# Scan tables of the next layer made by another engine, small vector instructions merged, and norm factors spread by transposes in a two-layer hybrid decoder kernel

## The chip, the cores and the metric

The kernel runs on one core of one Trainium2 chip. The metric is the device time of one execution in microseconds (us); less is better. TensorE (PE) multiplies matrices, VectorE (DVE), ScalarE (ACT) and GpSimd (POOL) work on tiles of up to 128 partitions, SyncE (SP) issues most transfers. Durations of single instructions are in nanoseconds (ns) where marked.

## The reference

The program is the trunk of a decoder with two layers, for one sequence of 512 tokens and a model width of 1024. Each layer adds to x a mixer and a feed-forward.

- The mixer projects RMSNorm(x) once, and slices of this projection feed three groups: six NSA heads (compressed, selected and windowed attention), six MLA heads, and a state-space scan (S5) with 16 groups of 16 channels and 64 complex states each. The groups are normed, concatenated and projected back.
- The feed-forward multiplies by an up matrix (1024 x 5632), convolves the gate half over three tokens, and multiplies by a down matrix (2816 x 1024).

What the change touches, cut down:

```python
def rms_norm(x, g):
    y = x * lax.rsqrt(jnp.mean(x * x, axis=-1, keepdims=True) + EPS)
    return y * g

def compress_blocks(blocks, pe, w1, b1, w2, b2):       # k and v of NSA, 31 blocks of 32 tokens
    h = gelu(einsum('bnlkd,ldf->bnkf', blocks + pe[:, None, :], w1) + b1)
    return einsum('bnkf,fd->bnkd', h, w2) + b2

def s5_ssm(u, log_dt, a_re, a_im, b_re, b_im, c_re, c_im, d, w_glu, b_glu):
    a_bar = exp(a * dt)                                # the scan tables hold powers of a_bar
    b_bar = ((a_bar - 1.0) / a)[..., None] * (b_re + 1j * b_im)
    h = scan(a_bar, einsum('bsgc,gpc->bsgp', u, b_bar))
    y = einsum('bsgp,gcp->bsgc', h, c).real + d * u
    z = gelu(y)
    return z * sigmoid(z @ w_glu + b_glu)

def conv_ffn(h, w_up, conv_w, conv_b, w_down):
    gate, val = split(h @ w_up, 2)
    gate = sum(pad(gate)[:, k:k + S] * conv_w[k] for k in range(3)) + conv_b
    return (silu(gate) * val) @ w_down
```

## The kernel before

Features lie on partitions and the 512 tokens on the free axis, so a projection tile is 128 features by 512 tokens in one PSUM bank. Each fp32 product is made of three passes (`mm3`, lines 240 to 242): a weight is split into a high part (a cast on ScalarE, line 226) and a low part (a subtraction on POOL or VectorE, line 227), and so is the activation. `wload` (line 234) loads a weight tile on SP's queue, with three raw buffers and four split ones.

In a layer the mixer's tasks (projections, the tables, the compression, the heads, the scan) are issued by a table (PLAN0 for layer 0, PLAN1 for layer 1), and the framework's scheduler makes each engine's final order from it, by its own estimate of times. An engine runs its instructions in that order. Tiles of 128x512 in SBUF come from an arena with three areas (main, side, aux) in which a name's number is a slot.

Names and lines that matter here:

- `rstd_` (to line 271) computes one norm factor for each token, as a column of 128 tokens for each of four blocks. It spreads each column over 128 partitions by a matmul of the column, broadcast, with the identity. `rstd_` is called 16 times, 14 times with four blocks and twice with two.
- `ssm_params` (lines 396 ff.) makes the scan's tables for a quarter of the scan's groups. Its complex product `cm` takes three lines: L425 (product with the real part), L426 (product with the imaginary part) and L427 (their sum), each 128x512. The tables of layer 0 are made inside its mixer; those of layer 1 in layer 0's feed-forward, two quarters in its first group (about 404 to 444 us) and two in its second (about 571 to 592 us).
- `ssm_spill` (lines 430 ff.) makes the convolution kernel of a quarter: transposes (L440), products (L447), a copy from PSUM by ScalarE (L451), and L453, which adds d on the diagonal of four 16x16 blocks.
- `compress` (for v) forms the gelu of the hidden layer six times over (L841, 128x31 each), multiplies by w2, adds a bias (L846) and multiplies by head masks (L850, 128x64 each).
- L519 are the score matmuls of a head, in four blocks of rows, L520 VectorE's instruction that takes a block out of its bank, adds the mask and finds the extremum of each row (with a short read of the accumulator behind it); the softmax scaling is L532 on POOL. L689 moves a projection from PSUM to SBUF.
- L680 and L683 write the scan's input u to DRAM and read it back in another arrangement, both on POOL's queue; L483 is the scan's first matmul on it.
- A feed-forward tile is 48 matmuls into two banks. VectorE moves the gate out (L1182), ScalarE and VectorE make the convolution (L1183 to L1185), ScalarE takes the silu (L1187), POOL multiplies by the norm factor (L1188), and VectorE by the value half (L1189). Two pairs of banks take turns.

```python
F.cur = ("aux",)
par = [ssm_params(l + 1, 2 * gi - 2 + q) for q in range(2)]
area("ffn")
```

## Time and profile before

| | |
|---|---|
| time, median of 3 runs | 1374.46 us (1372.62 to 1374.56) |
| span of the profiled execution | 1372.3 us |
| PE busy | 1302.4 us (95%) |
| VectorE busy | 856.5 us (62%) |
| POOL busy | 724.4 us (53%) |
| ScalarE busy | 638.8 us (47%) |
| chain that ended last | PE 72%, VectorE 19%, issue 3%, POOL 2%, ACT 2%, DMA 2% |

The profiled execution has its span, 1372.3 us, and no other time of its own; the median of the runs is 2.16 us above it. The chain is followed back from the last instruction to whatever released each step, so an engine's share there is time in which it was what the rest waited for.

### The profile page before, as it was taken

To read this page: it belongs to the slowest core of one execution; us is meant where nothing else is said; L and a number is where in the kernel's file an instruction comes from. 1 tells how busy PE (TensorE), PEld (TensorE's weight loads), DVE (VectorE), ACT (ScalarE), POOL (GpSimd) and SP (SyncE) were. 2 spreads that over 40 slices of the span, in tenths; PEclk is the share of its full clock that TensorE was granted. 3 is DMA by queue.
4 is the path that set the end of the run, shared out by engine and by line. 5 is a ranking of instruction groups with operands and counts; after the bars stand their busy time and mean duration, and the time that the engine had idled before them with its cause. 6 is when DMAs were issued, how large, how long until landed. Compare 5 with 4: busy or idle time off the path is not lost.

```text
span 1372.3 us, 19205 instructions
## 1 busy us (share of the span) xinstructions
PE 1302.4 (95%) x6414; PEld 1079.2 (79%) x6414; DVE 856.5 (62%) x1733; ACT 638.8 (47%) x1322; POOL 724.4 (53%) x722
## 2 busy tenths in 40 slices
PE   7888989998998999999999999999999999999997
PEld 5676777786876888888888887877878888888886
DVE  6988889858695334643466488986764433442455
ACT  4334667754443233423443356886453323332344
POOL 7485546654759155545437665556376315612532
PEclk9989999999999999999999999999999999999998
DMA  6243622212333333443353433121223333333332
GB/s 224 83 131 99 182 85 66 68 62 64 98 99 113 111 95 100 117 124 95 112 173 112 149 124 106 59 60 43 83 85 106 95 100 99 94 92 106 95 94 83
DMA packets 91556, 140.14 MB, mean 102 GB/s; under 512 B 15553, under 2 KB 36545, under 8 KB 91457
## 3 DMA queue, kind: packets, MB, share of 16 engines
q1 hardware_dynamic: 90176, 134.72, 32.2%
q0 software_dynamic: 1280, 4.20, 1.0%
q8 instruction: 50, 0.82, 0.3%
q14 instruction: 50, 0.40, 0.1%
HBM read 125.01 MB, written 15.96 MB: 103 GB/s over the span
## 4 chain that ended last, share of the span: by engine, by line
PE 72%; DVE 19%; issue 3%; POOL 2%; ACT 2%; DMA 2%; SPq 0%; DVEq 0%; POOLq 0%; ACTq 0%
PE bank L240 21%; PE bank L241 20%; PE bank L242 20%; DVE r L227 3%; PE bank L519 2%; PE bank L548 2%; DVE f L520 2%; PE bank L544 2%; DVE r L230 1%; DVE f L304 1%; DVE f L1157 1%; PE bank L271 1%; PE bank L816 1%; PE bank L253 1%; POOL wt L227 1%
## 5 line engine op out<-in xcount | busy, mean ns | idle before, releaser
L240 PE MATMUL bank<-r,wt 128*128 128x512 f32 x1466 | 580.9, 397 | 15.2 <-ACT wt L226 7.3
L241 PE MATMUL bank<-r,wt 128*128 128x512 f32 x1466 | 577.0, 394 | 4.4 <-DVE r L230 3.6
L242 PE MATMUL bank<-r,wt 128*128 128x512 f32 x1466 | 573.4, 394 | 5.1 <-POOL wt L227 5.1
L227 POOL TENSOR_TENSOR wt<-raw,wt 128x512 fp32r<-128x512 f32 (+2 forms) x272 | 355.0, 1309 | 300.1 <-ACT wt L226 291.0
L226 ACT CAST wt<-raw 128x512 fp32r<-128x512 f32 (+2 forms) x398 | 231.0, 584 | 332.5 <-PE bank L241 189.6
L240 PEld LDWEIGHTS bank<-r,wt 128*128 128x128 f32 x1466 | 278.2, 190 | 77.2 <-ACT wt L226 8.9
L242 PEld LDWEIGHTS bank<-r,wt 128*128 128x128 f32 x1466 | 278.0, 190 | 66.1 <-POOL wt L227 8.5
L241 PEld LDWEIGHTS bank<-r,wt 128*128 128x128 f32 x1466 | 278.4, 190 | 62.8 <-DVE r L230 6.5
L227 DVE TENSOR_TENSOR wt<-raw,wt 128x512 fp32r<-128x512 f32 (+3 forms) x126 | 88.9, 709 | 51.7 <-ACT wt L226 51.3
L294 POOL TENSOR_TENSOR f<-f,f 128x512 f32<-128x512 f32 (+1 forms) x53 | 68.0, 1284 | 99.9 <-ACT f L286 98.4
L532 POOL TENSOR_SCALAR f<-f,sml 128x128 f32<-128x128 f32 (+3 forms) x144 | 79.3, 569 | 52.2 <-DVE sml L530 18.0
L227 DVE TENSOR_TENSOR r<-bank,r 128x256 fp32r<-128x256 f32 (+4 forms) x196 | 90.2, 476 | 24.2 <-ACT r L226 23.0
L1182 DVE TENSOR_TENSOR f<-bank,f 128x512 f32<-128x512 f32 x44 | 30.3, 690 | 112.6 <-PE bank L242 103.1
L1188 POOL TENSOR_TENSOR f<-f,f 128x512 f32<-128x512 f32 x44 | 58.0, 1320 | 74.6 <-ACT f L1187 74.6
L523 ACT ACTIVATE f<-f,sml 128x384 f32<-128x384 f32 (+3 forms) x144 | 80.6, 560 | 32.5 <-DVE sml L520 31.6
L226 ACT CAST r<-bank 128x256 fp32r<-128x256 f32 (+4 forms) x196 | 79.0, 417 | 31.8 <-PE bank L544 15.7
L548 PE MATMUL bank<-r,r 128*128 128x512 f32 (+3 forms) x288 | 82.1, 353 | 10.4 <-DVE r L227 7.5
L519 PE MATMUL bank<-r,r 128*128 128x128 f32 (+3 forms) x336 | 79.3, 339 | 9.8 <-DVE sml L520 9.5
L226 ACT CAST r<-f 128x512 fp32r<-128x512 f32 (+1 forms) x76 | 46.9, 620 | 80.5 <-DVE f L1189 65.7
L520 DVE CUSTOM_DVE_ANT_0 f<-bank,cst 128x384 f32<-128x384 f32 (+3 forms) x144 | 67.8, 481 | 12.7 <-PE bank L519 11.6
L1189 DVE TENSOR_TENSOR f<-bank,f 128x512 f32<-128x512 f32 x44 | 30.4, 690 | 72.7 <-POOL f L1188 68.9
L1217 DVE TENSOR_TENSOR f<-bank,f 128x512 f32<-128x512 f32 x48 | 32.7, 688 | 65.6 <-PE bank L242 65.5
(225 smaller groups left out, 1549.9 us busy)
## 6 DMA issues: line engine op xcount, KB each, us to landing
raw<-in_wup_dram SPq DMA_DIRECT2D x176, 256.0 KB
raw<-in_wdn_dram SPq DMA_DIRECT2D x72, 256.0 KB
raw<-in_win_dram SPq DMA_DIRECT2D x64, 256.0 KB
f<-pd SPq DMA_DIRECT2D x32, 256.0 KB
raw<-in_wout_dram SPq DMA_DIRECT2D x32, 192.0 KB
f<-in_xT_dram SPq DMA_DIRECT2D x16, 256.0 KB
f<-in_w_dram SPq DMA_DIRECT2D x16, 256.0 KB
pd<-f SPq DMA_DIRECT2D x16, 256.0 KB
```

What stands on the lines that cost most here:

```text
L226: A.copy(hi, src)
L227: (E or V).tensor_tensor(lo, src, f32(hi), op=OP.subtract)
L240: PE.matmul(p, lhsT=w[:, 0, o:o + n], rhs=x[:, 0], start=start, stop=False)
L241: PE.matmul(p, lhsT=w[:, 0, o:o + n], rhs=x[:, 1], start=False, stop=False)
L242: PE.matmul(p, lhsT=w[:, 1, o:o + n], rhs=x[:, 0], start=False, stop=stop)
L294: G.tensor_tensor(a, a, q, op=OP.add)
L519: PE.matmul(p[:, :w], lhsT=q[:, i * 128:w], rhs=k[:, :w], start=n == 0, stop=n == len(passes) - 1)
L520: V.tensor_tensor_reduce(out=sm[i], in0=p[:, :w], in1=C("mask")[:, 512 - w:], op0=OP.add, op1=OP.min, scale=1.0, scalar=3.0e38, accum_out= ...
L523: A.activation(sm[i], sm[i], AF.Exp, bias=mx[:, i:i + 1], scale=-1.0, accum_out=su[:, i:i + 1])
L532: G.tensor_scalar(sm[i], sm[i], rs[:, i:i + 1], 1.0, op0=OP.mult, op1=OP.mult)
L548: PE.matmul(o[:, j * 128:], lhsT=v[j], rhs=pr[:, x, :w], start=first and j == 0 and x == 0, stop=last and j == 3 and x == 1)
L1188: G.tensor_tensor(t, t, r_f, op=OP.mult)
```

## The change

There are four parts.

1. In `rstd_` the matmul of the broadcast column with the identity is written as a transpose of the same operands.
2. In `ssm_params` the tables of layer 1 go from POOL to VectorE (L425, L426 and L427, 24 instructions of 128x512). For layer 0 the engines stay as they were: L425 on POOL, L426 and L427 on VectorE.
3. In `ssm_spill` the four 16x16 multiply-adds L453 become one product of 16x4x16 into a tile of its own (L455, which needs nothing but constants and parameters) and one add of 16x4x16 (L457).
4. In `compress` six 128x31 instructions become one of 128x62 and two copies that repeat it three times, and six 128x64 products become one of 128x4x64 and one of 128x2x64.

A comment ahead of PLAN0 is taken out, which does nothing. The line numbers of the kernel after are four higher than before from L456 on, and five higher from about L851 on.

```diff
--- before.py
+++ after.py
@@ -268,7 +268,7 @@
         V.scalar_tensor_tensor(y, t, 5.0, y, op0=OP.add, op1=OP.mult)
         p = ps(ring)
         for i in range(nb):
-            PE.matmul(p[:, i * 128:(i + 1) * 128], lhsT=y[:, i:i + 1].to_broadcast([128, 128]), rhs=ident, start=True, stop=True)
+            PE.transpose(p[:, i * 128:(i + 1) * 128], y[:, i:i + 1].to_broadcast([128, 128]), ident)
         if keep:
             return p
         r = F.get()
@@ -394,7 +394,7 @@
         ssm_par[l] = dict(ar=ar, ai=ai, ais=ais, r8=r8, cr=cr, c2=c2)
 
     def ssm_params(l, q):
-        E2 = V if l == 0 else G
+        E1 = G if l == 0 else V
         P = ssm_par[l]
         g0 = q * 4
         sv = F.get()
@@ -422,9 +422,9 @@
             def pw(p):
                 return p[:, :, g0:g0 + 4].rearrange("p k g -> p g k")[:, :, :, None].to_broadcast(sh4)
             ov, tv = shp(o, 4, 8, 16), shp(tmp, 4, 8, 16)
-            G.tensor_tensor(ov, a[:, :, None, :].to_broadcast(sh4), pw(pa), op=OP.mult)
-            E2.tensor_tensor(tv, b[:, :, None, :].to_broadcast(sh4), pw(pb), op=OP.mult)
-            E2.tensor_tensor(o, o, tmp, op=OP.add)
+            E1.tensor_tensor(ov, a[:, :, None, :].to_broadcast(sh4), pw(pa), op=OP.mult)
+            V.tensor_tensor(tv, b[:, :, None, :].to_broadcast(sh4), pw(pb), op=OP.mult)
+            V.tensor_tensor(o, o, tmp, op=OP.add)
 
         X, O1 = F.get(), F.get()
         cm(X, bb, P["ar"][:, 0:8, :], bs, P["ais"])
@@ -449,9 +449,13 @@
                       rhs=O1[:, g * 128:g * 128 + 112], start=True, stop=True)
         F.free(sv)
         A.copy(kt[0:16], pk[0:16])
-        for g in range(4):
-            V.scalar_tensor_tensor(kt[0:16, g * 128:g * 128 + 16], ident[0:16, 0:16], S(l, "ssd", g0 + g)[0:16],
-                                   kt[0:16, g * 128:g * 128 + 16], op0=OP.mult, op1=OP.add)
+        kd0 = shp(kt[0:16], 4, 128)[:, :, 0:16]
+        dg = F.get()
+        dv = shp(dg[0:16], 4, 16)
+        V.tensor_tensor(dv, ident[0:16, 0:16][:, None, :].to_broadcast([16, 4, 16]),
+                        S(l, "ssd")[0:16, g0:g0 + 4][:, :, None].to_broadcast([16, 4, 16]), op=OP.mult)
+        V.tensor_tensor(kd0, kd0, dv, op=OP.add)
+        F.free(dg)
         SY.dma_start(kd[l, :, g0:g0 + 4, 0:112], zt[:, None, :].to_broadcast([16, 4, 112]))
         SY.dma_start(kd[l, :, g0:g0 + 4, 112:240], shp(kt[0:16], 4, 128))
         for i, x in enumerate((I1, O1)):
@@ -836,9 +840,9 @@
                 hr = F.get()
                 hrep = shp(hr, 8, 32)
                 G.memset(hr[:, 0:256], 0.0)
-                for r in range(6):
-                    c = slice(31 * (r // 3), 31 * (r // 3) + 31)
-                    V.scalar_tensor_tensor(hrep[:, r, 0:31], a[:, c], 1.0, hy[:, c], op0=OP.add, op1=OP.mult)
+                V.scalar_tensor_tensor(hy, a, 1.0, hy, op0=OP.add, op1=OP.mult)
+                for g in range(2):
+                    V.tensor_copy(hrep[:, 3 * g:3 * g + 3, 0:31], hy[:, 31 * g:31 * g + 31][:, None, :].to_broadcast([128, 3, 31]))
                 for b in range(2):
                     PE.matmul(p[:, b * 64:b * 64 + 64], lhsT=hr[:, b * 128:(b + 1) * 128], rhs=w2, start=True, stop=True)
                 F.free(hr)
@@ -846,8 +850,9 @@
                 V.tensor_tensor(vb, shp(p, 2, 64), S(l, "cvb2")[:, None, :].to_broadcast([128, 2, 64]), op=OP.add)
                 vmt = F.get()
                 vm = shp(vmt, 6, 64)
-                for h in range(6):
-                    V.tensor_scalar(vm[:, h, :], vb[:, h // 4, :], C("hm", h), None, op0=OP.mult)
+                for h0, n in ((0, 4), (4, 2)):
+                    V.tensor_tensor(vm[:, h0:h0 + n, :], vb[:, h0 // 4, :][:, None, :].to_broadcast([128, n, 64]),
+                                    C("hm")[:, h0:h0 + n][:, :, None].to_broadcast([128, n, 64]), op=OP.mult)
                 split(vm, vc[:, :, 0, :], vc[:, :, 1, :])
                 F.free(vmt)
             F.free(sx)
```

The scheduler orders the rows of each engine anew. Three places follow. A row has the line, the instruction, what it writes and reads, and its shape; `f_` are arena tiles, `bank_` PSUM banks, `sml_` small columns, `r_` and `wt_` split activations and weights.

On VectorE in layer 0's mixer, before: the four L453 of a quarter stand ahead of the last mask addition of a head (L520) and of the evacuation of a projection (L689).

```order
L227 TENSOR_TENSOR r_110<-bank_155,r_110 128x4x64
L520 ISA f_69,sml_145<-bank_153,cst 128x384
L520 ISA sml_145 128x1
L453 SCALAR_TENSOR_TENSOR f_91<-cst,smt,f_91 16x16 x4
L520 ISA f_71,sml_145<-bank_154,cst 128x512
L520 ISA sml_145 128x1
L427 TENSOR_TENSOR f_95<-f_95,f_97 128x512
L689 TENSOR_TENSOR f_72<-bank_151,f_79 128x512
```

The same place after:

```order
L227 TENSOR_TENSOR r_110<-bank_155,r_110 128x4x64
L524 ISA f_69,sml_145<-bank_153,cst 128x384
L524 ISA sml_145 128x1
L457 TENSOR_TENSOR f_91<-f_91,f_92 16x4x16
L524 ISA f_71,sml_145<-bank_154,cst 128x512
L524 ISA sml_145 128x1
L416 TENSOR_SCALAR f_95<-f_95,cst 128x64
L426 TENSOR_TENSOR f_92<-f_95,ais 128x512
L693 TENSOR_TENSOR f_72<-bank_151,f_79 128x512
```

The four L453 have become one L457 behind the same mask addition (L524 is L520 before); between the next one and the evacuation, L693, two table rows (L416 and L426) stand where L427 stood.

On VectorE in layer 0's feed-forward, before: one tile from its first evacuation (L1182) to its multiply (L1189) and split.

```order
L1182 TENSOR_TENSOR f_63<-bank_154,f_74 128x512
L1184 SCALAR_TENSOR_TENSOR f_68<-f_63,smt,f_68 128x511
L1185 SCALAR_TENSOR_TENSOR f_68<-f_63,smt,f_68 128x510
L1189 TENSOR_TENSOR f_68<-bank_151,f_68 128x512
L227 TENSOR_TENSOR r_123<-f_68,r_123 128x512
```

After: the multiply of this tile is L1194, the last of these rows, and its first evacuation, L1187 into `f_63`, stands six rows ahead of the first of them, with L416, L426, L417, L227 and one L425 between.

```order
L425 TENSOR_TENSOR f_81<-f_87,ar 128x512
L427 TENSOR_TENSOR f_78<-f_78,f_83 128x512
L1189 SCALAR_TENSOR_TENSOR f_68<-f_63,smt,f_68 128x511
L426 TENSOR_TENSOR f_82<-f_87,ais 128x512
L426 TENSOR_TENSOR f_83<-f_79,ai 128x512
L1190 SCALAR_TENSOR_TENSOR f_68<-f_63,smt,f_68 128x510
L427 TENSOR_TENSOR f_81<-f_81,f_82 128x512
L427 TENSOR_TENSOR f_85<-f_85,f_83 128x512
L426 TENSOR_TENSOR f_82<-f_87,ai 128x512
L455 TENSOR_TENSOR f_83<-cst,smt 16x64
L427 TENSOR_TENSOR f_80<-f_80,f_82 128x512
L1194 TENSOR_TENSOR f_68<-bank_151,f_68 128x512
```

Ten of the moved table instructions stand now between the two (L426 and L425 ahead of these rows, eight in them), and one L455.

On POOL in layer 0's mixer, before: the read L683 of the scan's input; its write, L680, stands 15 rows higher.

```order
L532 TENSOR_SCALAR f_81<-f_81,sml_150 128x128
L532 TENSOR_SCALAR f_74<-f_74,sml_150 128x256
L532 TENSOR_SCALAR f_81<-f_81,sml_150 128x384
L532 TENSOR_SCALAR f_75<-f_75,sml_150 128x512
L425 TENSOR_TENSOR f_89<-f_90,ar 128x512
L683 DMA f_95<-ud_175 128x512
L532 TENSOR_SCALAR f_76<-f_76,sml_133 128x128
```

After: the write (L684) and the read (L687) stand directly behind one another.

```order
L536 TENSOR_SCALAR f_86<-f_86,sml_133 128x256
L536 TENSOR_SCALAR f_76<-f_76,sml_133 128x384
L536 TENSOR_SCALAR f_87<-f_87,sml_133 128x512
L684 DMA ud_175<-f_95 128x8x64
L687 DMA f_93<-ud_175 128x512
L536 TENSOR_SCALAR f_73<-f_73,sml_136 128x128
L536 TENSOR_SCALAR f_80<-f_80,sml_136 128x256
```

The read has moved to behind the scalings of the next head, and the write with it.

## Rows read from the trace of the kernel before

**Rows 1.** Stretches of the span: busy us of each engine (instructions), granted clock, DMA share, GB/s.

```profile
90.00:120.00 30.00, 25.65 (x129) 20.78 (x129) 26.37 (x58) 10.72 (x25) 21.97 (x33) 0.90 0.30 92
160.00:330.00 170.00, 157.00 (x874) 130.61 (x872) 133.47 (x377) 113.50 (x291) 88.04 (x112) 0.97 0.24 73
404.00:444.00 40.00, 36.51 (x153) 28.25 (x152) 25.46 (x33) 15.46 (x27) 38.54 (x36) 0.99 0.40 118
560.00:600.00 40.00, 40.00 (x203) 32.80 (x202) 26.39 (x38) 13.77 (x23) 23.23 (x27) 1.00 0.48 136
788.00:815.00 27.00, 27.00 (x156) 23.52 (x155) 21.39 (x68) 15.32 (x43) 17.77 (x24) 1.00 0.45 143
```

**Rows 2.** PE's timeline: start, us, instruction, idle time before it and its releaser.

```profile
118.59 0.80 PE L519 MATMUL bank<-r,r 128*128 128x256 f32 x2 [3.11 <-DVE sml L520]
...
120.39 0.63 PE L241 MATMUL bank<-r,wt 128*128 128x512 f32 x1
...
124.99 0.39 PE L240 MATMUL bank<-r,wt 128*128 128x512 f32 x1
```

**Rows 3.** VectorE's timeline in layer 0's mixer.

```profile
94.41 3.95 DVE L841 SCALAR_TENSOR_TENSOR f<-f 128x31 f32<-128x31 f32 x6
...
103.18 3.07 DVE L850 TENSOR_SCALAR f<-f,cst 128x64 f32<-128x64 f32 x6
...
111.50 0.34 DVE L416 TENSOR_SCALAR f<-f,cst 128x64 f32<-128x64 f32 x1 [2.77 <-DMA f<-in_sc_dram]
...
114.63 3.29 DVE L453 SCALAR_TENSOR_TENSOR f<-cst,smt,f 16x16 f32<-16x16 f32 x4
```

**Rows 4.** POOL's timeline in the same stretch.

```profile
115.44 1.09 POOL L425 TENSOR_TENSOR f<-f,ar 128x512 f32<-128x512 f32 x1
116.50 1.25 POOL L227 TENSOR_TENSOR wt<-raw,wt 128x512 fp32r<-128x512 f32 x1
```

**Rows 5.** Durations by source line: ns min/median/max, first and last start.

```profile
L453 DVE SCALAR_TENSOR_TENSOR f<-cst,smt,f x32: 216/223/1290, 114.6 to 692.8; 16x16 f32<-16x16 f32 x32
...
L425 POOL TENSOR_TENSOR f<-f,ar x16: 1092/1110/1705, 82.7 to 585.8; 128x512 f32<-128x512 f32 x16
...
L426 DVE TENSOR_TENSOR f<-f,ais x4: 628/984/1740, 89.4 to 126.1; 128x512 f32<-128x512 f32 x4
...
L427 DVE TENSOR_TENSOR f<-f,f x8: 675/684/1367, 91.3 to 140.3; 128x512 f32<-128x512 f32 x8
L427 POOL TENSOR_TENSOR f<-f,f x8: 1268/1458/1746, 424.0 to 591.4; 128x512 f32<-128x512 f32 x8
```

**Rows 6.** PE's waits, 120 to 160 us: total us, times, longest.

```profile
PE bank L519 <- DVE sml L520: 1.8, 1, 1.8
```

**Rows 7.** PE's waits, 404 to 446 us.

```profile
PE bank L242 <- POOL wt L227: 1.8, 4, 0.7
PE bank L240 <- DVE f L1189: 0.9, 1, 0.9
```

**Rows 8.** VectorE's timeline in the feed-forward of layer 0, one tile.

```profile
416.20 0.68 DVE L1182 TENSOR_TENSOR f<-bank,f 128x512 f32<-128x512 f32 x1
...
418.81 1.48 DVE L1185 SCALAR_TENSOR_TENSOR f<-f,smt,f 128x510 f32<-128x510 f32 x1
424.05 0.69 DVE L1189 TENSOR_TENSOR f<-bank,f 128x512 f32<-128x512 f32 x1 [3.77 <-PE bank L242]
```

**Rows 9.** L271 and L1004 on PE: ns min/median/max; PE's timeline behind L1004.

```profile
L271 PE MATMUL bank<-cst,sml x120: 270/275/582, 34.5 to 1365.4; 128*128 128x128 f32 x120
...
L1004 PE MATMUL bank<-cst,f x16: 270/272/292, 130.7 to 786.1; 128*128 128x128 f32 x16
...
785.34 1.06 PE L1004 MATMUL bank<-cst,f 128*128 128x128 f32 x8
...
786.93 0.40 PE L241 MATMUL bank<-r,wt 128*128 128x512 f32 x1
```

**Rows 10.** The scan input's write to DRAM (L680), time from issue to landing.

```profile
DMA to landing us min/median/max: 3.7/4.1/4.7
```

## The prediction

> **What bounds the kernel now.** I read the page's totals first: TensorE (PE) is busy 95% of the 1372.3 us span and stands on 72% of the chain that ended last, VectorE (DVE) on 19%, GpSimd (POOL) on 2%. A change can therefore gain only in the stretches where PE is not full, and there only if it shortens what PE waits for. The next view is the table of stretches [rows 1]: PE is idle 4.35 us of 30 in the stretch 90 to 120 us (layer 0's projections, tables and first heads) with DVE busy 26.37 of 30, 13.0 us of 170 in the rest of layer 0's mixer, and 3.49 of 40 at 404 to 444 us (first group of layer 0's feed-forward, where the next layer's tables are made), there with POOL busy 38.54 of 40. It is idle nowhere at 560 to 600 us (the second place of those tables) and 788 to 815 us (layer 1's compression). So three of the change's places are worth reading, and two are not.
>
> The first place, by PE's timeline [rows 2]: a score matmul L519 stood 3.11 us for VectorE's L520, and right behind it the fp32 matmuls, which start 0.23 us apart at the full 2.4 GHz, run at half of it: from 120.39 to 124.99 eleven of them take 4.60 us, 0.42 each. Eleven at 0.23 would take 2.5, so the slow stretch costs some 2.1 us more, and the whole stop about 5.2. VectorE's timeline says why L520 was late [rows 3]: four 16x16 L453 held the engine 3.29 us, from 114.63 on. One L453 takes 0.223 us in the median and 1.29 at most [rows 5]; POOL's timeline has its two 128x512 instructions, 1.09 and 1.25 us, exactly there [rows 4], so the third and fourth L453 stood while POOL ran. The Trainium skill, page "SBUF — State Buffer", section "Who interferes with whom", has a rule for it: a VectorE instruction with two SBUF inputs and a GpSimd instruction that reads SBUF share a port pair, and whoever has it keeps it for its whole instruction. The trace agrees: 3.29 us for four instructions of 0.22.
>
> **The change part by part.**
>
> *Spill diagonal (four L453 become a product placed early and one add behind the copy).* What stays at the critical place is one 16x4x16 add. Its price is not in the trace; below it lies a lone L453 (0.22), above it one that meets a POOL instruction (1.29) [rows 5]; I take 0.9, between them and nearer the upper, as POOL's table product still runs there. 3.29 - 0.9 = 2.4 us come off the wait of 3.11, which leaves 0.7; a stop that short should not bring the half clock (the 0.9 us wait at 413 us [rows 7] lies in a stretch granted 0.99), so most of the 2.1 goes too. Gain 2.4 + 2.1 = 4.5; bounds 0 (something else is late in its stead) to 5.2 (all of it). The three later quarters of layer 0 give back something of the 1.8 us that L519 waits for L520 at 120 to 160 us [rows 6]; I take 1.0, bounds 0 and 1.8. The extra tile costs an arena slot and one product of a few tenths, which lies before the copy that the add waits for.
>
> *Compression (twelve small instructions become five, per layer).* In layer 0 L841 falls from 3.95 us to three instructions and L850 from 3.07 to two [rows 3]. Each new one lies between 0.22 (the smallest instruction of rows 5) and 0.68 (a whole 128x512, L427), so 0.7 to 2.0 and 0.4 to 1.4; some 4.5 us of VectorE are saved. But behind both, at 111.50, VectorE sat idle 2.77 us until a load of the table's inputs had landed [rows 3]. The time saved ahead of that becomes more idle time there. I count 0, bounds 0 and -2. In layer 1 PE is full at 788 to 815 us: 0.
>
> *Tables of layer 1 from POOL to VectorE (24 instructions of 128x512, six per quarter, two quarters in each of two stretches).* On POOL one takes 1.11 (L425) to 1.46 us (L427) [rows 5], so 12 of them give back 13 to 17 of the 38.54 us that POOL is busy at 404 to 444. That is where PE waits four times, 1.8 us in all, for POOL's half of the weight split [rows 7]; this wait I take as gone. On VectorE one takes 0.68 (L427) to 0.98 (L426, its median beside POOL) [rows 5], 8.2 to 11.8 us onto 25.46 of 40: it still fits, but not evenly. By the order rows, ten of the twelve now stand between one tile's first evacuation L1187 (L1182 before) and its last multiply L1194 (L1189 before). Before, those lay 424.05 - 416.20 = 7.85 us apart, of which VectorE was idle 3.77 for POOL's part [rows 8], though the row puts it down to PE. Now VectorE has there its own L1182, L1184 and L1185 (0.68, about 1.0, 1.48 [rows 8]) and 6.8 to 9.8 us of tables: 10.0 to 13.0, with the last multiply 10.6 to 13.6. Banks go by pairs, so the tile after next wants this bank one tile (48 matmuls at 0.227 = 10.9 us) and six matmuls (1.4 us) behind this tile's last matmul: 12.3 us. PE thus waits 0 to 1.3 us for it where it waited 0 before; with the small rows between, up to 2.7. I take 1.0. Sum of the place: -1.8 + 1.0 = -0.8; bounds -2.7 (the 0.9 for L1189 [rows 7] vanishes as well) and +0.9. In the second stretch PE is full and VectorE busy 26.39 of 40 [rows 1], POOL is relieved there too: 0, and +1 at worst.
>
> *Norm factors by transposes.* Sixty broadcast matmuls (120 records, 0.275 us each) become transposes, which this kernel already has: L1004, 0.272 [rows 9]. Nothing is gained or lost by duration: 120 x 0.003 = 0.4 us at most. The skill's "TensorE: Matmul & The Clock Gate", Part 4 on the transpose mode, speaks against this part: a transpose does not count as work for the clock. By that, matmuls behind each of the 14 large calls could run at half clock. The trace does not agree for runs of this length: behind eight L1004 in a row at 785.34 a matmul has 0.40 us in the records [rows 9], as at full speed (0.39; 0.63 at half [rows 2]).
>
> **Sum.** Against the profiled span: 1372.3 - 4.5 - 1.0 - 0.8 = 1366.0. The runs' median, 1374.46, lies 2.16 above that span (the kernel's time has that much around the profiled one), so 1368.2 us.
>
> **Rivals.**
> *More is gained.* Other waits of layer 0's mixer end on VectorE too (13 us of PE idle at 160 to 330 [rows 1]); if the seven us that VectorE loses at 94 to 149 us arrive there, or the compression is not swallowed by the load, some 3 to 8 us more: about 1362. Against it: that idle time is in many short waits.
> *Nothing is gained.* The stop at 118 us only changes its name: either the last multiply of a projection or the scan's input comes late. The order shows a candidate: the write of the scan's input to DRAM and its read back (the write takes 4.1 us to land, and the read has to wait for it [rows 10]) now stand directly behind each other in POOL's queue and later than before, so POOL stands some 4 us and its softmax scalings with it; a PE wait of 3 us with 2.1 of half clock takes back the 5.5. Time 1374.
> *Slower: VectorE becomes the bound in the feed-forward.* If the moved instructions take 1.3 us rather than 0.7 to 1.0 (as L427 at its longest, 1.37 [rows 5], when POOL's splits hold them up), ten take 13.0 and the last multiply ends 16.9 us behind the first evacuation: 4.6 late, in two tiles 9.2, with 2.1 of half clock each 13.4. Against the gain of 5.5 + 1.8: 1374.46 + 6.1 = 1380.6. It decides from some 3.7 us of wait per tile on. For it: the crowding in the order; against: VectorE's short rows at 404 to 444 mostly ran at 0.7.
> *Slower: the clock falls behind the transposes.* By the rule of Part 4, 14 calls x 2.1 us = 29 us less the gain, about 1397; that the row of the eight L1004 shows full speed behind them stands against it.
>
> **How the numbers follow.** No gain or loss under 0.2% (2.75 us, about what a measurement of this kernel can tell from no change) counts. The forecast, 1364.5 to 1371.5, has a chance of 0.48; more gained 0.17; nothing gained (1371.7 to 1377.2) 0.21; VectorE bound 0.11; clock 0.03. Faster 0.48 + 0.17 + 0.02 (cases of nothing that end a little below) = 0.67; same 0.19; slower 0.14. Likeliest 1368.2; 8 in 10 need both neighbours: 1360.5 (the larger gain's middle and some) to 1376.0, which leaves out some 0.06 below and 0.14 above.
>
> **What the profile after would show.** L519's wait at 118 us at or under 1 us and no half-clock matmuls at 120 to 125; the L457 adds under 1 us; no PE wait for POOL's weight split at 404 to 446 and POOL busy about 24 of 40 there, VectorE about 35; PE full at 560 to 600 and 788 to 815; L271 still 0.27 us with full matmuls behind. Wrong if L1194 shows as PE's releaser in the feed-forward for over 3 us, if the scan's first matmul L487 waits for a DRAM read, or if a new wait of 2 us or more stands between 110 and 160 us.

## The result and the profile after

| | before | changed |
|---|---|---|
| time, median | 1373.54 us (1372.4 to 1374.56) | 1384.91 us (1382.1 to 1386.0) |
| span of the profiled execution | 1372.3 us | 1383.6 us |
| granted clock over the span | 0.985 | 0.977 |
| PE, VectorE, POOL busy | 1302.4, 856.5, 724.4 us | 1301.8, 866.6, 699.4 us |

The ratio is 1.008 [1.0066, 1.0094]: slower by 11 us, where 6 less were forecast (1368.2 for 1374.46). Now and then an execution ran at a lower granted clock and took far longer (one of e1 below: 1464.86 us at 0.84); such executions are in no ratio, and the trace of e1 is of that one. The chain that ended last now reads, on the page of the changed kernel:

```profile
PE 73%; DVE 17%; issue 3%; ACT 3%; DMA 2%; POOL 1%; SPq 0%; DVEq 0%; ACTq 0%; POOLq 0%
```

A ruler through the two programs is the feed-forward's multiply (L1189 before, L1194 after): both kernels run it 44 times in the same order, so the start of each, less that of its like before, says by how much the kernel is late there.

| start before, us | 368 | 413 | 424 | 439 | 498 | 686 | 1035 | 1330 |
|---|---|---|---|---|---|---|---|---|
| changed kernel, us late | +7.8 | +9.5 | +15.0 | +7.7 | +11.2 | +10.7 | +12.0 | +12.0 |

The loss arises in two places: ahead of 368 us (layer 0's mixer, about 8) and between 368 and 498 us (first group of the feed-forward, 3.4). From 498 us on hardly anything is added. The same stretches as in [rows 1], after:

```profile
90.00:120.00 30.00, 25.87 (x132) 21.62 (x132) 22.18 (x46) 10.88 (x24) 19.09 (x29) 0.85 0.28 92
160.00:330.00 170.00, 151.57 (x819) 125.52 (x818) 131.71 (x375) 108.42 (x279) 86.83 (x110) 0.94 0.25 75
404.00:444.00 40.00, 30.18 (x120) 22.98 (x120) 36.84 (x52) 13.68 (x24) 29.22 (x27) 0.91 0.37 111
560.00:600.00 40.00, 40.00 (x203) 32.76 (x203) 26.37 (x42) 14.96 (x25) 14.37 (x19) 1.00 0.42 118
788.00:815.00 27.00, 27.00 (x151) 23.38 (x150) 18.21 (x53) 14.10 (x38) 17.58 (x23) 1.00 0.42 126
```

At 404 to 444 us POOL was relieved (38.54 to 29.22, forecast about 24), but PE ran 6.3 us less. The stretches are of fixed times and the changed kernel is about 8 us late in this one, so not all of the 6.3 belongs to the change there (see the feed-forward below). The two stretches where PE was full are full still.

**Layer 0, 85 to 93 us.** VectorE's timeline of the changed kernel:

```profile
84.99 0.43 DVE L311 TENSOR_SCALAR f<-f 128x512 f32<-128x512 f32 x1
85.45 6.96 DVE L1052 TENSOR_TENSOR r<-f,r 64x512 fp32r<-64x512 f32 x1
92.44 0.69 DVE L693 TENSOR_TENSOR f<-bank,f 128x512 f32<-128x512 f32 x1
93.04 0.35 DVE L983 TENSOR_TENSOR f<-bank,cst 128x192 f32<-128x192 f32 x1
```

POOL's timeline in the same stretch:

```profile
85.09 1.44 POOL L227 TENSOR_TENSOR r<-f,r 64x512 fp32r<-64x512 f32 x1
86.50 1.27 POOL L227 TENSOR_TENSOR wt<-raw,wt 128x512 fp32r<-128x512 f32 x1
...
88.23 2.15 POOL L425 TENSOR_TENSOR f<-f,ar 128x512 f32<-128x512 f32 x2
90.33 0.30 POOL L842 MEMSET f<- 128x256 f32 x1
90.60 1.26 POOL L227 TENSOR_TENSOR wt<-raw,wt 128x512 fp32r<-128x512 f32 x1
91.82 0.76 POOL L415 TENSOR_TENSOR f<-f 128x64 f32<-128x64 f32 x1
```

And the waits of PE from 80 to 104 us, the changed kernel:

```profile
PE bank L981 <- DVE f L983: 4.3, 1, 4.3
PE bank L820 <- DVE r L1052: 3.7, 1, 3.7
```

L1052 is the second low part of k (L1047 before). VectorE's timeline of the kernel before has it at the same place with 0.69 us:

```profile
84.73 0.69 DVE L1047 TENSOR_TENSOR r<-f,r 64x512 fp32r<-64x512 f32 x1 [0.16 <-ACT r L226]
```

In the changed kernel it started while POOL was at work and ended after 6.96, at 92.41, when POOL was nearly through its row of instructions, which stand back to back. PE then waited 4.3 us for what was queued behind it (L983). The 3.7 us of the view are no part of this: that wait ended at 81.15 us, ahead of the stall, behind an earlier L1052 (79.44 us, 1.70 long). Before, the same view has one wait only, 2.9 us for a load.

The stall is not the whole of layer 0's loss. PE's waits (the rows of the view added up) and the granted clock, by stretches:

| stretch, us | 60 to 110 | 110 to 150 | 150 to 250 | 250 to 375 |
|---|---|---|---|---|
| before | 8.8 us, 0.90 | 6.7 us, 0.91 | 6.7 us, 0.97 | 7.6 us, 0.99 |
| changed | 11.7 us, 0.83 | 3.7 us, 0.96 | 10.0 us, 0.93 | 10.7 us, 0.97 |

Where the stall is, PE waits 2.9 us more than before; where the spill's stop was, 3.0 less; behind 150 us 6.4 more, in many waits of at most 2.4 us each.

**The spill diagonal, where the gain was forecast,** went by halves: VectorE's timeline has `L457` at 117.55 us, 0.21 long, and PE's wait of 3.11 us is gone. But what is late next is the evacuation of a projection, and the half clock is there behind it. PE's timeline of the changed kernel:

```profile
121.61 0.50 PE L240 MATMUL bank<-r,wt 128*128 128x512 f32 x1 [2.30 <-DVE f L693]
122.96 0.63 PE L242 MATMUL bank<-r,wt 128*128 128x512 f32 x1
```

**The feed-forward.** VectorE's timeline of one tile, changed kernel:

```profile
423.04 0.68 DVE L1187 TENSOR_TENSOR f<-bank,f 128x512 f32<-128x512 f32 x1
424.27 0.83 DVE L416 TENSOR_SCALAR f<-f,cst 128x64 f32<-128x64 f32 x1 [0.56 <-DMA f<-in_sc_dram]
425.02 0.86 DVE L426 TENSOR_TENSOR f<-f,ais 128x512 f32<-128x512 f32 x1
425.80 1.28 DVE L417 TENSOR_SCALAR f<-f 128x64 f32<-128x64 f32 x1
...
429.73 1.78 DVE L1189 SCALAR_TENSOR_TENSOR f<-f,smt,f 128x511 f32<-128x511 f32 x1
431.43 1.78 DVE L426 TENSOR_TENSOR f<-f,ais 128x512 f32<-128x512 f32 x1
...
433.73 0.74 DVE L1190 SCALAR_TENSOR_TENSOR f<-f,smt,f 128x510 f32<-128x510 f32 x1
...
437.28 1.27 DVE L455 TENSOR_TENSOR f<-cst,smt 16x64 f32<-16x64 f32 x1
438.48 0.67 DVE L427 TENSOR_TENSOR f<-f,f 128x512 f32<-128x512 f32 x1
439.08 0.67 DVE L1194 TENSOR_TENSOR f<-bank,f 128x512 f32<-128x512 f32 x1
```

ScalarE's timeline there:

```profile
434.56 0.63 ACT L1192 ACTIVATE f<-f 128x512 f32<-128x512 f32 x1 [5.83 <-DVE f L1190]
435.10 0.60 ACT L226 CAST wt<-raw 128x512 fp32r<-128x512 f32 x1
```

PE's waits, 404 to 450 us:

```profile
PE bank L240 <- DVE f L1194: 4.8, 2, 3.3
PE bank L242 <- POOL wt L227: 3.2, 2, 2.3
PE bank L240 <- ACT wt L226: 1.8, 1, 1.8
```

From the first evacuation to the last multiply it is 439.08 - 423.04 = 16.0 us, where it was 7.85 [rows 8]. The silu stands 5.83 us for the late convolution, and behind it in ScalarE's order the cast of the next weights, for which PE waits 1.8 us. Of the 3.2 us for POOL's split, 2.3 are a wait that the kernel before has too, ahead of the window of [rows 7]. PE's timeline before, and of the changed kernel:

```profile
400.38 0.50 PE L242 MATMUL bank<-r,wt 128*128 128x512 f32 x1 [2.28 <-POOL wt L227]
407.94 0.50 PE L242 MATMUL bank<-r,wt 128*128 128x512 f32 x1 [2.27 <-POOL wt L227]
```

So the wait for POOL's split that was to vanish fell from 1.8 to 0.9 us, and longer ones came beside it. Together PE waits 7.5 us, in place of 3.4 before (the 2.7 of [rows 7] and 0.7 for an activation's split).

### The profile page after: what moved, and what is told of

Read it like the earlier page. It is cut to its first block, busy times and chain, and to the rows that moved or that the text cites. A ratio compares the mean times of both kernels' runs of the same rounds, so it can differ in the third digit from the quotient of the medians.

```text
span 1383.6 us, 19070 instructions
## 1 busy us (share of the span) xinstructions
PE 1301.8 (94%) x6354; PEld 1077.4 (78%) x6354; DVE 866.6 (63%) x1727; ACT 639.2 (46%) x1322; POOL 699.4 (51%) x698
## 4 chain that ended last, share of the span: by engine, by line
PE 73%; DVE 17%; issue 3%; ACT 3%; DMA 2%; POOL 1%; SPq 0%; DVEq 0%; ACTq 0%; POOLq 0%
PE bank L240 21%; PE bank L241 21%; PE bank L242 21%; PE bank L523 2%; PE bank L552 2%; DVE r L227 2%; PE bank L548 2%; DVE r L230 1%; DVE f L524 1%; DVE f L304 1%; DVE f L1162 1%; ACT r L226 1%; PE bank L253 1%; DMA f<-in_sc_dram 1%; PE bank L820 1%
## 5 line engine op out<-in xcount | busy, mean ns | idle before, releaser
L227 POOL TENSOR_TENSOR wt<-raw,wt 128x512 fp32r<-128x512 f32 (+2 forms) x272 | 356.1, 1313 | 322.6 <-ACT wt L226 318.2
L240 PEld LDWEIGHTS bank<-r,wt 128*128 128x128 f32 x1466 | 279.5, 191 | 90.9 <-ACT wt L226 10.7
L227 DVE TENSOR_TENSOR wt<-raw,wt 128x512 fp32r<-128x512 f32 (+3 forms) x126 | 84.2, 672 | 47.1 <-ACT wt L226 47.0
L227 DVE TENSOR_TENSOR r<-bank,r 128x256 fp32r<-128x256 f32 (+4 forms) x196 | 91.0, 476 | 31.3 <-ACT r L226 26.6
L1187 DVE TENSOR_TENSOR f<-bank,f 128x512 f32<-128x512 f32 x44 | 30.4, 690 | 110.7 <-PE bank L242 102.0
L552 PE MATMUL bank<-r,r 128*128 128x512 f32 (+3 forms) x288 | 85.1, 361 | 15.0 <-DVE r L227 7.9
L527 ACT ACTIVATE f<-f,sml 128x512 f32<-128x512 f32 (+3 forms) x144 | 80.9, 562 | 29.5 <-DVE sml L524 27.9
L1222 DVE TENSOR_TENSOR f<-bank,f 128x512 f32<-128x512 f32 x48 | 32.8, 689 | 70.5 <-PE bank L242 70.4
L524 DVE CUSTOM_DVE_ANT_0 f<-bank,cst 128x512 f32<-128x512 f32 (+3 forms) x144 | 68.2, 483 | 12.9 <-PE bank L523 12.0
L552 PEld LDWEIGHTS bank<-r,r 128*128 128x128 f32 x288 | 51.8, 194 | 31.4 <-DVE r L227 15.5
```

The costliest lines, as they stand in the source:

```text
L227: (E or V).tensor_tensor(lo, src, f32(hi), op=OP.subtract)
L240: PE.matmul(p, lhsT=w[:, 0, o:o + n], rhs=x[:, 0], start=start, stop=False)
L524: V.tensor_tensor_reduce(out=sm[i], in0=p[:, :w], in1=C("mask")[:, 512 - w:], op0=OP.add, op1=OP.min, scale=1.0, scalar=3.0e38, accum_out= ...
L527: A.activation(sm[i], sm[i], AF.Exp, bias=mx[:, i:i + 1], scale=-1.0, accum_out=su[:, i:i + 1])
L552: PE.matmul(o[:, j * 128:], lhsT=v[j], rhs=pr[:, x, :w], start=first and j == 0 and x == 0, stop=last and j == 3 and x == 1)
```

## The experiments

The theories at the start were that the loss lies at those two places and comes from the parts that put VectorE late there (A in the expectations for the feed-forward, B for layer 0), or else that any edit at all costs this kernel some microseconds, because the scheduler orders everything anew (C in the expectations), or that the transposes slow the clock. Two more were made on the way: a clash with the spill's transfers (D), and the arena tile of the merge (E). Each kernel is the one before with the edit shown, timed beside the kernel before; parts are numbered as in the section on the change.

| run | edit | median, us | ratio to before |
|---|---|---|---|
| e1_tables | part 2 | 1379.14 | 1.0039 [1.0024, 1.0054] |
| e2_transposes | part 1 | 1378.42 | 1.0038 [1.0025, 1.0052] |
| e3_merges | parts 3, 4 | 1376.6 | 1.0026 [1.0013, 1.004] |
| e4_no_tables | parts 1, 3, 4 | 1383.13 | 1.0071 [1.0054, 1.0088] |
| e5_null | one memset more per norm factor | 1375.57 | 1.0013 [0.9998, 1.0027] |
| e6_copy | L1047 as a copy on ScalarE | 1376.71 | 1.0013 [1.0002, 1.0025] |
| e7_copy_transposes | part 1 and that copy | 1375.73 | 1.0016 [1.0003, 1.0029] |
| e8_second_tables | part 2, second group alone | 1374.86 | 1.0007 [0.9997, 1.0017] |
| e9_all_copy | all parts and the copy | 1379.22 | 1.0049 [1.0037, 1.0061] |
| e10_repaired | e9 with e8's tables | 1377.72 | 1.0039 [1.0027, 1.0051] |
| e11_few_tables | four L425 of part 2 | 1375.88 | 1.0023 [1.0011, 1.0036] |
| e12_spill_merge | part 3 | 1379.93 | 1.005 [1.0038, 1.0062] |
| e13_spill_light | part 3, lighter transfers | 1374.88 | 1.0014 [1.0001, 1.0027] |
| e14_before_light | lighter transfers | 1367.14 | 0.996 [0.9947, 0.9974] |
| e15_compress | part 4 | 1369.69 | 0.9978 [0.9966, 0.9991] |
| e16_spill_own_tile | part 3, tile of its own | 1368.65 | 0.9964 [0.9951, 0.9977] |
| e17_merges_own_tile | e16 and part 4 | 1368.04 | 0.9964 [0.9951, 0.9978] |
| e18_all_repaired | e10 with e16's tile | 1367.54 | 0.9946 [0.9928, 0.9965] |

### The parts apart: e1 to e4

```diff
# e1, part 2 alone (L426 and L427 too)
-            G.tensor_tensor(ov, a[:, :, None, :].to_broadcast(sh4), pw(pa), op=OP.mult)
+            E1.tensor_tensor(ov, a[:, :, None, :].to_broadcast(sh4), pw(pa), op=OP.mult)
# e2, part 1 alone
-            PE.matmul(p[:, i * 128:(i + 1) * 128], lhsT=y[:, i:i + 1].to_broadcast([128, 128]), rhs=ident, start=True, stop=True)
+            PE.transpose(p[:, i * 128:(i + 1) * 128], y[:, i:i + 1].to_broadcast([128, 128]), ident)
# e3: parts 3 and 4; e4: parts 1, 3 and 4, as in the change's diff
```

> Only the tables of layer 1 go to VectorE; layer 0's mixer keeps its rows. Theory A (VectorE becomes the bound in the first group of the feed-forward, ScalarE's weight casts wait behind it): PE again waits 3 us or more for the multiply of a tile and the kernel is 4 to 6 us slower than before (about 1378 to 1380). Rival (the loss there is a late effect of layer 0's new order): within 2 us of before.

> Only the broadcast matmuls become transposes. Theory B (the loss of some 6.5 us in layer 0 comes from the new order of rows that this part alone sets off, with a VectorE subtraction held up behind a run of POOL instructions): 3 to 8 us slower. Rival 1 (layer 0's loss belongs to the merged instructions): within 2 us of before. Rival 2 (the clock falls behind transposes): half-clock matmuls behind every L271, 10 us or more slower.

> Only the merges in the spill and the compression. Theory B: the wait of 3.11 us for L453 is gone as forecast and the kernel is 2 to 6 us faster than before. Rival 1 (layer 0's loss belongs to the merges): 3 to 8 us slower.

> The change without the move of the tables. Theories A and B together: 5 us faster than the change, 6 to 7 us slower than before (about 1380), with layer 0 as in the change. Rival (layer 0's loss is not bound to these parts): within 2 us of before.

Every part costs something: by the ratios 5.4 us the tables, 5.2 the transposes, 3.6 the two merges, 9.8 all but the tables. e1 and e2 came out as theories A and B had it, e3 as its rival; e4 missed, for it was to be 5 us faster than the change and is 1.8 (1383.13 against 1384.91). No row of e1's trace is shown. In e2 VectorE's timeline has the stall of L1047 with no other part there:

```profile
85.31 6.97 DVE L1047 TENSOR_TENSOR r<-f,r 64x512 fp32r<-64x512 f32 x1
```

e4 has it too (6.99 us at its longest), e3, which keeps the matmuls, has not (1.77). So the order made anew with the transposes puts L1047 beside POOL's busiest row. That this is where e2 loses its 5 us, its trace does not show: by the ruler (further below) it is level with before from 368 to 498 us and late only by 1035 us. The clock rival would have cost some 29 us; 5 is no sign of it.

### Is any new order dear, and does the stall explain part 1: e5 to e7

```diff
# e5
         v, t, y, h = sml(nb), sml(nb), sml(nb), sml(nb)
+        V.memset(v, 0.0)
# e6, and e7 with part 1
-                    V.tensor_tensor(kk[d0:d0 + 64, 1], f, f32(kk[s0:s0 + 64, 0]), op=OP.subtract)
+                    A.copy(kk[d0:d0 + 64, 1], f32(kk[s0:s0 + 64, 1]))
```

> The kernel before with one more memset of 128x4 on VectorE in each of the 16 norm factors (some 0.06 us each, 1 us in all, mostly hidden), which sets off a new order of the rows on every engine. Theory C (the order of before suits the chip unusually well and any new order costs some us, whatever the edit is for): 3 to 10 us slower than before. Rival (the losses belong to the edits themselves): within 2 us of before.

> Control for the next: the kernel before with the second low part of k (L1047, VectorE with two inputs in SBUF) copied by ScalarE instead. No stop at 85 us to remove here; within 3 us of before, either way.

> The transposes alone, with that copy on ScalarE. Theory B (what the transposes cost is the 7 us for which L1047 is shut out behind POOL at 85 us): within 2 us of the control e6, and 3 to 5 us faster than the transposes alone. Rival (the transposes cost by their place on TensorE or by other rows): 3 us or more slower than the control.

e5 cannot be told from no change, but it is no test of theory C: in the traces PE's rows stand as before up to 930 us, and of VectorE's only 12 stand elsewhere beside the added ones. What speaks against C, as a toll on every new order, are e6 and e18 (below), in whose traces 359 and 295 of PE's 6414 rows have moved: e6 costs 1.8 us (by the ratio), and e18 is faster than before. That a wider reordering tends to cost, whatever the edit is for, is not excluded: the changed kernel and the eight runs in which over 430 of PE's rows moved (e2, e3, e4, e7, e9, e10, e12, e13) are all slower than before.

e6 is the control for e7. With the copy, part 1 costs nothing more (1.0016 beside 1.0013), and e7 is 3.0 us faster than e2 by the ratios, as theory B had it. So the stall of L1047 is likely the price of part 1. It is not shown beyond doubt: the intervals of e2 and e7 touch, and the copy brings a new order of its own.

### Where the tables cost: e8, e11

```diff
# e8
-        E2 = V if l == 0 else G
+        E1, E2 = (G, V) if l == 0 else (V, V) if q >= 2 else (G, G)
# e11
+        E1, E2 = (G, V) if l == 0 else (V, G) if q < 2 else (G, G)
```

> Only the tables of the second group of the feed-forward go to VectorE; those of the first stay on POOL. Theory A (the loss of the tables is made by the crowding in the first group alone): within 2 us of before, TensorE full at 560 to 600 us. Rival (both places lose): 2 to 4 us slower.

> Before, with only the first group's four products L425 on VectorE (two of them between a tile's first evacuation and its multiply, where the change has ten). Theory A (it is the number of VectorE instructions ahead of the multiply that decides): TensorE waits no longer than before for the multiply, time within 1.5 us of before or a little less. Rival (any of the tables on VectorE costs, by the port it shares with POOL): 2 us or more slower.

The second group's twelve cannot be told from free. All 24 less these twelve is 1.0039 - 1.0007, so 4.4 us for the first group; the changed kernel's ruler has 3.4 there. Moving only four instructions there (e11) still costs 3.1 us: here theory A, by which the number of moved instructions decides, missed, and the rival (any of them costs) had the time, though its reason, the port, was not tested. ScalarE's timeline has the same picture, a silu that stands for VectorE (2.14 us before, at 420.38) with the casts behind it.

```profile
421.01 0.63 ACT L1187 ACTIVATE f<-f 128x512 f32<-128x512 f32 x1 [5.95 <-DVE f L1185]
421.55 1.12 ACT L226 CAST wt<-raw 128x512 fp32r<-128x512 f32 x2
```

### The change with its two repairs: e9, e10

The edits are e6's copy in the whole change (e9), and with e8's line in place of part 2 (e10).

> The whole change, with the second low part of k copied by ScalarE. Theories A and B: layer 0 loses no longer, the feed-forward still does: some 5 us faster than the change, 5 to 7 us slower than before (1378 to 1381). Rival (layer 0's loss is spread over its new order, not in the one stop): within 2 us of the change (1383 to 1386).

> Transposes, merges and that copy, with only the second group's tables on VectorE. Theories A and B: both losses are gone; within 2 us of before (1372 to 1376). Rival: still 4 us or more slower than before.

e9 came out as expected: it loses 6.7 us where the whole change lost 11, so the copy gives back 4 to 5 net. e10 was to come out level with before and is 5 us above it. Something in parts 3 and 4 was still unexplained.

### Part 3 by itself: e12 to e15

```diff
# e12: part 3 as in the change; e15: part 4 as in the change
# e13 (with part 3) and e14 (without): four strided transfers of the spill become one plain one
-        for g in range(4):
-            src = kd[l, :, g0 + g, 0:128]
-            src = bass.AP(tensor=src.tensor, offset=src.offset, ap=[[16, 8], list(src.ap[0]), [1, 128]])
-            SY.dma_start(pd[l][q][:, 3, g * 128:(g + 1) * 128], src)
+        SY.dma_start(pd[l][q][:, 3, :], O1)
```

> The spill's merge alone. Forecast of the prediction: the 3.11 us stop at 118 us goes, and 4 to 6 us are gained. Theory D (the stop goes, but layer 0's new order has other stops of its own): the stop is gone from the trace and the time is within 2 us of before.

> The compression's merges alone. Forecast of the prediction: nothing gained or lost, within 2 us of before. Rival (they cost like the spill's merge): 3 us or more slower.

> The spill's merge alone, with the four small strided transfers per quarter that arrange the convolution kernel (L466, 512-byte rows) replaced by one plain 256 KB transfer of another tile, so that the scan's result is not the reference's. Theory D (the time gained at 118 us is lost at 159 us, where a load of in_win stands behind the scan tables' transfers and ScalarE's cast of it holds up the casts behind it): the load lands earlier, ScalarE's idle time of 6.1 us ahead of that cast falls by 2 us or more, and the kernel is 3 us or more faster than the spill's merge alone. Rival (layer 0 loses it at other places): within 2 us of the spill's merge alone.

> Control for e13: the kernel before with the same plain transfer. Theory D: gains less than e13 does over the spill's merge alone, 0 to 3 us, since there the load was nearly hidden.

Part 4 alone gains 3.0 us (0.9978), so the whole loss of e3 is part 3's: 6.9 us by itself, though the stop at 118 us is gone in it; neither the forecast nor theory D had that. In e12 ScalarE's timeline shows a weight cast that stands 6.11 us for its load at 158.62 us, where it stood 2.54 before, which made the spill's transfers suspect (before, then e12):

```profile
158.64 0.63 ACT L226 CAST wt<-raw 128x512 fp32r<-128x512 f32 x1 [2.54 <-DMA raw<-in_win_dram]
158.62 0.62 ACT L226 CAST wt<-raw 128x512 fp32r<-128x512 f32 x1 [6.11 <-DMA raw<-in_win_dram]
```

e13 and e14 copy another table in place of the convolution kernel's strided read, so that part of the scan is left out in both. e13 by itself came as theory D had it, 4.9 us faster than e12 with that wait at 3.13 us, but its control gains as much. With light transfers part 3 stays 1374.88 - 1367.14 = 7.7 us behind the kernel without it. The light transfers give both kernels 5 to 6 us, so they are not the cause: theory D falls.

### The tile: e16 to e18

```diff
+    dgs = [mk([16, 64], f"dg{i}") for i in range(2)]
...
-        dg = F.get()
-        dv = shp(dg[0:16], 4, 16)
+        dv = shp(dgs[q % 2], 4, 16)
...
-        F.free(dg)
```

(against part 3 as the change writes it; e17 adds part 4; e18 adds part 4, part 1, the copy of e6 and e8's line.)

> The spill's merge alone, with its product in two small tiles of its own instead of an arena tile; TensorE's order then stays that of before in all but a few rows. Theory E (the arena tile that the merge borrows shifts the tiles of everything behind it, and the new order that follows loses what the merge gains): the stop at 118 us is gone and the kernel is 3 to 6 us faster than before, 10 us faster than the merge with the arena tile. Rival (what is gained at 118 us is given back in layer 0's heads in any order): within 2 us of before.

> Both merges, the spill's with its own small tiles. Theory E: the gains of the compression alone (3 us) and of e16 add up: 6 to 9 us faster than before (1364 to 1367). Rival: no better than the compression's merges alone (1369 to 1371).

> All four parts, each mended: transposes with ScalarE's copy of the low part of k, both merges with the spill's own small tiles, and only the second group's tables on VectorE. Theories A, B and E: the merges' gain remains and nothing else costs, 1367 to 1371, 7 us or more faster than the same kernel with the arena tile (e10). Rival (the arena tile matters only in the order of before, the transposes' order loses it anyway): 1375 or more.

The same instructions on two small tiles of their own, in place of a 128x512 tile borrowed from the arena, turn 6.9 us slower into 5.0 us faster. Against before, 10 of PE's 6414 rows stand elsewhere in the trace with the own tile, and 472 with the borrowed one (rows compared by line, tiles without their numbers, and shape). VectorE's timeline of e16, with the add between the same two mask additions:

```profile
114.31 0.92 DVE L457 TENSOR_TENSOR f<-f,dg 16x64 f32<-16x64 f32 x1
115.16 0.67 DVE L523 CUSTOM_DVE_ANT_0 f<-bank,cst 128x512 f32<-128x512 f32 x1
```

PE's timeline of e16 behind it:

```profile
115.90 0.51 PE L522 MATMUL bank<-r,r 128*128 128x256 f32 x2 [0.74 <-DVE sml L523]
118.77 0.80 PE L241 MATMUL bank<-r,wt 128*128 128x512 f32 x1 [2.37 <-DVE f L692]
119.37 0.63 PE L242 MATMUL bank<-r,wt 128*128 128x512 f32 x1
```

The add took the 0.92 us and the wait the 0.74 that the prediction put there (0.9 and 0.7). The half clock did not go away, though: a wait of 2.37 us for a projection's evacuation follows, and the records behind it are 0.63 us, as at half clock [rows 2]. What was gained beside the wait came further on: 160 to 250 us is granted 1.00 in e16 and 0.96 before.

e17 stays below the 6 to 9 us that were expected, and e18 came out as expected. The ruler for these kernels and two earlier ones, us against before:

| start before, us | 368 | 413 | 498 | 1035 | 1330 |
|---|---|---|---|---|---|
| e2_transposes | -0.3 | -0.5 | -0.6 | +2.7 | +2.7 |
| e11_few_tables | -2.7 | -0.4 | +0.0 | -0.1 | -0.1 |
| e9_all_copy | +2.0 | +3.7 | +4.6 | +5.8 | +5.8 |
| e10_repaired | +2.1 | +1.9 | +2.5 | +2.6 | +2.5 |
| e12_spill_merge | +3.5 | +3.3 | +3.9 | +4.4 | +4.4 |
| e15_compress | -1.8 | -1.6 | -1.6 | -1.9 | -1.9 |
| e16_spill_own_tile | -6.6 | -6.3 | -6.4 | -5.8 | -5.8 |
| e17_merges_own_tile | -5.3 | -5.0 | -5.1 | -5.9 | -5.9 |
| e18_all_repaired | -6.6 | -6.9 | -7.0 | -5.4 | -5.4 |

The ruler is of one execution each, and executions of one kernel lie some microseconds apart (e18: 1362.77 to 1368.23), so its single rows are good to 2 or 3 us. Nearly all gains and losses of parts 3 and 4 are made ahead of 368 us. e18 has everything that the change wanted, but the first group's tables, and beats both kernels: 0.9946 [0.9928, 0.9965] of the kernel before, 7.4 us by the ratio (the medians, 1367.54 and 1372.34, lie 4.8 apart). e17, without transposes, copy and tables, is at 0.9964; the intervals of the two overlap.

## Why the prediction was wrong, step by step

- **Spill diagonal, -4.5 and -1.0.** The mechanism was right: e16 is 5.0 us faster, with the add and the wait as worked out. The sizes agree in part by luck. The add took 0.92 us in e16 but 0.26 in e12 and 0.21 in the changed kernel. That the half clock would go with the wait was wrong, and PE's waits at 110 to 160 us fell by 1.3 us only (6.7 before, 5.4 in e16); the rest was gained later in the mixer. The 1.0 for the later quarters no run shows apart. The L453 that POOL held up were the first three (0.87, 1.13 and 1.29 us), not the third and fourth. The step that failed is "The extra tile costs an arena slot and one product of a few tenths". The slot cost 1379.93 - 1368.65 = 11.3 us (e12 against e16, the same instructions): tiles got other slots and the engines another order, and the mixer lost more than the merge gave. The prediction priced the tile by the instruction that fills it and not by who else wants the slot, although arena and scheduler stand in the description of the kernel.
- **Norm factors, 0.** "Nothing is gained or lost by duration" was priced by duration alone. The step that failed is the silent one that the order around it stays. The new order put L1052 beside a full row of POOL instructions, where it took 6.96 us in place of 0.69. Part 1 alone lost 5 us (e2), and nothing beside its control with that instruction off VectorE (e7 beside e6); that the stall made the 5 us is likely, not shown. The 0.4 us by duration were too small as well: half of the records are gone, and PE is busy with L271 for 9.7 us in place of 17.0, which in time is not to be seen. The clock rival was false. PE's timeline of the changed kernel, behind four transposes L271 of a norm factor:

```profile
743.28 0.60 PE L271 MATMUL bank<-cst,sml 128*128 128x128 f32 x4
743.63 0.48 PE L240 MATMUL bank<-r,wt 128*128 128x512 f32 x1
743.95 0.39 PE L242 MATMUL bank<-r,wt 128*128 128x512 f32 x1
744.18 0.40 PE L240 MATMUL bank<-r,wt 128*128 128x512 f32 x1
```

The products behind them have the 0.39 us of full speed, as behind the L1004 [rows 9]. The Trainium skill, page "TensorE: Matmul & The Clock Gate", Part 4, says that a transpose does not count as work for the clock. Behind these four it cost nothing.

- **Tables in the feed-forward, -0.8, bounds -2.7 and +0.9.** The rival came true: multiply's end 439.08 + 0.67 - 423.04 = 16.7 us behind the evacuation (rival 16.9), PE waiting for L1194 twice, 4.8 us (rival 9.2, with half clock 13.4). But its reason was not the one given. The ten moved instructions took 9.3 us together in that tile, inside the 6.8 to 9.8 of the forecast. The term that failed is "with the small rows between, up to 2.7", which leaves these rows 1.4 us: L416, L417, L227 and L455 took 0.83 + 1.28 + 0.68 + 1.27 = 4.1 us; L455 alone took 1.27 beside POOL, where its shortest is 0.20. The wait for POOL, taken as gone, went by half (1.8 to 0.9 us). And a new one of 1.8 us came, since ScalarE's weight casts stand behind the silu that is now late; that consequence was in no step. The sum was 3.4 to 4.4 us, not -0.8.
- **Second group's tables, 0; layer 1's compression, 0.** Right (e8; full stretches).
- **Compression, 0.** The bound of -2 was passed: 3.0 us gained (e15), as the rival that more is gained had it for this part. The claim that the load at 111.50 us swallows it is half borne out: in e15 VectorE still stands there, 1.88 us in place of 2.77.
- **Nothing gained, by the write and read of the scan's input.** POOL stood 4.5 us between the two, as this rival had it, but PE did not: the scan's first matmul (L487) waits once in the whole span, 0.6 us, for ScalarE. What did come of the rival is its other half, the projection that is late instead: 2.30 us for L693 in the changed kernel, 2.37 for L692 in e16. It is also the wait of 2 us or more between 110 and 160 us that the prediction named as a sign of being wrong.

The parts do not add. Part 4 gains 3.0 us alone, and next to nothing on top of e16 (e17: 5.6 where 8 would be the sum). What stays open: by which rows the borrowed slot loses its 11 us. From 150 to 250 us PE's waits add up to 11.5 us in e12, 6.7 before and 7.1 in e16, the longest single one in e12 is 1.6 us; 200 to 210 us is granted 0.68 in it (0.83 before). The loss is spread over many short waits and half-clock stretches, and no run forced the old order onto the borrowed slot. Also open are why four moved instructions (e11) cost nearly as much as twelve, and how much of layer 0's 8 us in the changed kernel is the stall's: the copy gives back 4 to 5 (e9).

## What to carry to other kernels

Where a scheduler or an arena places work, price an edit also by what it displaces: here a small buffer of its own kept the order (10 of PE's rows moved) and the gain, a slot of the shared arena moved 472 and lost it. Before an order is trusted, look for two-input VectorE instructions that now stand beside a dense run of POOL, and in a tile's path count all rows in between, not only the moved ones. Then ask what is queued behind the late one on the next engine: here a weight cast behind a silu stopped TensorE for 1.8 us.

## What the runs showed of the hardware

- A VectorE instruction with two SBUF inputs, 0.69 us by itself, took 6.96 while POOL ran its instructions without a gap (6.97 in e2). The Trainium skill, page "SBUF — State Buffer", section "Who interferes with whom", says that whoever holds the shared port pair keeps it for its instruction. The trace agrees so far that the VectorE instruction was long where POOL ran, but it lasted over nearly the whole run of POOL instructions, of which the longest single one is 1.44 us.
- A broadcast matmul of the norm factor made two records of 0.275 us (120 for 60 calls [rows 9]), the transpose one. The lines view of the changed kernel:

```profile
L271 PEld LDWEIGHTS bank<-cst,sml x60: 133/135/232, 33.8 to 1376.6; 128*128 128x128 f32 x60
L271 PE MATMUL bank<-cst,sml x60: 270/272/473, 34.0 to 1376.8; 128*128 128x128 f32 x60
```

The records of a call overlap: PE's busy time on L271 falls from 17.0 to 9.7 us. In time this is not to be seen (e7 beside e6).
